# Remainders of the float32r splits on another engine in the attention phases, and query stacks built by copies

## The chip, the cores and the metric

One core of a Trainium2 chip runs the whole program. The metric is the device time of one execution in microseconds; the kernel before takes 1898.29 us (median of three runs, 1894.59 to 1900.06).

## What is computed

Two layers of a transformer trunk. Each layer has 512 latent and 256 context tokens of width 1024, one input projection whose columns go to four head groups (A: windowed attention with a sink, B: differential attention, C: retention in both directions, D: neighbourhood attention on a grid), one output projection, and a squared-ReLU MLP. Shift, scale and gate of every norm come from a linear map of the condition.

```python
hx = rms_norm(x, p['norm1_g']) * (1 + sc1x) + sh1x
(lw_q, ..., ln_v) = split_in(hx @ p['w_in'])          # the same for the context tokens
out_w = window_attention(q, k, v, k_c, v_c, p['a_sink'])
out_f = rms_norm(diff_attention(q, k, v, k_c, v_c, lam), p['b_subln_g']) * (1 - lambda_init)
out_r = rms_norm(o_f + flip(o_b), p['c_gn_g']) * gate
out_n = neighbourhood_attention(q, k, v, k_c, v_c, p['d_rpb'])
x = x + g1x * (concatenate([out_w, out_f, out_r, out_n]) @ p['w_out'])
h2 = rms_norm(x, p['norm2_g']) * (1 + sc2x) + sh2x
x = x + g2x * (square(relu(h2 @ p['w_mlp1'])) @ p['w_mlp2'])
```

The second layer has no outputs for the context tokens, so its queries and its MLP run over 512 columns in place of 768.

## The kernel before, in words

Activations lie transposed in SBUF, features on partitions and tokens on columns, 768 to a tile. TensorE multiplies in float32r, a rounded form of float32, so a float32 operand is split into a rounded part `hi` and a remainder `lo`, and a product takes three matmuls: hi x hi, hi x lo, lo x hi (L315 to L317 in `gemm`). `split` (L274) makes the two: ScalarE copies the source into `hi` (L275), VectorE subtracts `hi` from the source into `lo` (L276). All callers of `split` share these two lines in the profile, so one tells them apart by the tiles: `wh`, `wl` for weights, `pth`, `ptl` for transposed probabilities, `sp` for group B's queries and keys, `oh`, `ol` for the attention outputs.

`wload` (L278) loads a 128x512 chunk of weights into `wr` (five buffers) on SP's queue, and splits it into `wh` and `wl` (four buffers each), with a priority 40 places ahead of the code around it. Every input tile has two chunks.

Queries and keys are stacked so that the parts lie above one another on the contraction axis. `qstack` (L594; groups A, C, D) puts a head's 64 rows of `hi` and 64 rows of `lo` into one tile: ScalarE writes one half (L599), VectorE the other (L600), both across partitions. `kstack` (L603) writes `hi` twice and `lo` twice: one half by ScalarE (L608) and VectorE (L610), the other half by a DMA from the first (`KCOPY`, L633, issued by SP at L634). Group B has four heads of 32 rows to a tile, and `stack32` (L617) splits the whole tile once and places all quarters by DMA, 16 copies to a stack.

A layer's attention consists of seven units, a0 b0 b1 c0 c1 d0 d1. A generator (`in_a` to `in_d`) yields a unit's input projections, another (`at_a` to `at_d`) its attention. `weave` (L106) runs through them: while a unit's attention is emitted, the projections of the next are mixed in, so far ahead as written in constants (`lead`, 0.25 to 0.6 of a unit). The first attention of a layer therefore follows its own projections directly, with a part of the next unit's projection emitted before it. `out_ac` (L1033), the output projection of six of the eight tiles, is the filling for the last unit. A scheduler takes what is emitted in order of priority and fixes the order on each engine when the kernel is built; at run time each engine and SP's queue work strictly in that order and wait at semaphores. All DMAs are issued by SP.

The tiles `zq` (five buffers of 128x768) hold what is short-lived: squares, a projection on its way, group B's `hi` and `lo`. `u3` (20 buffers) holds stacks and outputs. GpSimd is used for nothing. `mods_dve` makes the condition's products on VectorE beside the MLP.

Of the kernel before, what the change touches and what calls it, by code (L numbers as in the profile page):

```python
# [9 lines left out]
F32 = mybir.dt.float32  # L10
F32R = mybir.dt.float32r
AF = mybir.ActivationFunctionType
OP = mybir.AluOpType
# [66 lines left out]
PTB = 2  # L80
PSB = 2
POB = 1
ZQ = 5
U3 = 20
MID = 14
WPRI = 40
# [67 lines left out]
@with_exitstack  # L154
def body(ctx: ExitStack, tc, A):
    nc = tc.nc
    V, S, G, T, SY = nc.vector, nc.scalar, nc.gpsimd, nc.tensor, nc.sync

    cons = ctx.enter_context(tc.tile_pool(name="cons", bufs=1))
    main = ctx.enter_context(tc.tile_pool(name="main", bufs=1))  # L160
# [6 lines left out]
    def nm(p):  # L167
        cnt[0] += 1
        return f"{p}{cnt[0]}"
# [18 lines left out]
    for w in (128, 64, 32):  # L188
        t = cons.tile([128, 32], F32, name=f"gmean{w}")
# [5 lines left out]
    with tc.tile_pool(name="sp0", bufs=1) as sp0:  # L195
        t = sp0.tile([128, 3, 128], F32, name="spread0")
# [74 lines left out]
            V.scalar_tensor_tensor(sq[:, s:s + l], ap, EPS if eps else 0.0, sq[:, s:s + l], op0=OP.add, op1=OP.mult)  # L271
        V.scalar_tensor_tensor(sq[:, :n], sq[:, :n], -3.0, e3[:, :n], op0=OP.add, op1=OP.mult)

    def split(src, hi, lo):  # L274
        S.activation(hi, src, AF.Copy)  # L275
        V.tensor_tensor(lo, src, hi.bitcast(F32), op=OP.subtract)  # L276

    def wload(src, k0=0, k1=8, dst=None):  # L278

        res = []  # L280
        for a in range(k0, k1, 4):
            n = min(4, k1 - a)
            r = wp.tile([128, 512], F32, name=nm("wr"), tag="wr", bufs=WR)[:, :128 * n]
            SY.dma_start(out=r, in_=src[:, 128 * a:128 * a + 128 * n])
            if dst is not None:
                hi, lo = dst
            else:
                hi = wp.tile([128, 512], F32R, name=nm("wh"), tag="wh", bufs=WB)
                lo = wp.tile([128, 512], F32R, name=nm("wl"), tag="wl", bufs=WB)
            with tc.high_priority(offset=WPRI):  # L290
                split(r, hi[:, :128 * n], lo[:, :128 * n])
            res += [(hi[:, 128 * k:128 * k + 128], lo[:, 128 * k:128 * k + 128]) for k in range(n)]
        return res

# [30 lines left out]
    def u3r(p):  # L325
        return main.tile([128, 768], F32R, name=nm(p), tag="u3", bufs=U3)
# [135 lines left out]
    for L in range(DEPTH):  # L462
        last = L == DEPTH - 1
        nq = NX if last else NT
# [2 lines left out]
        rb = rowb[:, L, :]  # L467
        modc = modcs[L]


        att = ExitStack()
        ap_ = att.enter_context(tc.tile_pool(name=f"att{L}", bufs=1))
        if L == 0:
# [34 lines left out]
            order = [(c[0], int(c[1])) for c in LOADS.split()]  # L508
            for c in order[:AHEAD]:
                load(*c)  # L510
            order = order[AHEAD:]
            h = htiles()
            gs = gstile()
            y = acc1
# [76 lines left out]

        HALF = (slice(0, 64), slice(64, 128))

        def qstack(t, n):  # L594

            st = (u3r("qs"), u3r("qs"))
            for h, x in enumerate(st):
                a, b = HALF[h], HALF[1 - h]
                S.activation(x[a, :n], t[a, :n], AF.Copy)  # L599
                V.tensor_tensor(x[b, :n], t[a, :n], x[a, :n].bitcast(F32), op=OP.subtract)  # L600
            return st

        def kstack(t, n):  # L603

            st, lo = (u3r("ks"), u3r("ks")), (u3r("kl"), u3r("kl"))
            for h, (x, y) in enumerate(zip(st, lo)):
                a, b = HALF[h], HALF[1 - h]
                S.activation(x[a, :n], t[a, :n], AF.Copy)  # L608
                KCOPY(x[b, :n], x[a, :n])
                V.tensor_tensor(y[a, :n], t[a, :n], x[a, :n].bitcast(F32), op=OP.subtract)  # L610
                KCOPY(y[b, :n], y[a, :n])
            return st, lo

        def quarter(i):
            return slice(32 * i, 32 * i + 32)

        def stack32(t, n, order):  # L617

            parts = [main.tile([128, 768], F32R, name=nm("sp"), tag="zq", bufs=ZQ)[:, :n] for _ in range(2)]
            split(t[:, :n], *parts)  # L620
            st = [u3r("st") for _ in range(4)]
            for i, x in enumerate(st):
                for r, w in enumerate(order):
                    KCOPY(x[quarter(r), :n], parts[w][quarter(i)])
            return st

        def qstack32(t, n):
            return stack32(t, n, (0, 1, 0, 1))

        def kstack32(t, n):  # L630
            return stack32(t, n, (0, 0, 1, 1))

        def KCOPY(dst, src):  # L633
            SY.dma_start(out=dst.bitcast(F32), in_=src.bitcast(F32))  # L634
# [260 lines left out]
        def ctables(hd):  # L895

            lf, nlb = lg[:, hd:hd + 1], nlg[:, 4 + hd:5 + hd]
            tb = grptile()
            tx = ap_.tile([128, 2, 512], F32, name=nm("tx"), tag="grp", bufs=GRP)
            SY.dma_start(out=tb[:, 0:896], in_=A['dd'][:, 0:896])  # L900
            SY.dma_start(out=tx.rearrange("p t i -> p (t i)"), in_=A['dd'][:, 896:1920])
            tn = zm()
            V.tensor_scalar(tn[:, 0:128], tb[:, 384:512], 0.0, lf, op0=OP.max, op1=OP.mult)
            V.tensor_scalar(tb[:, 384:512], tb[:, 384:512], 0.0, nlb, op0=OP.min, op1=OP.mult)
            V.tensor_tensor(tb[:, 384:512], tb[:, 384:512], tn[:, 0:128], op=OP.add)
            S.activation(tb[:, 384:512], tb[:, 384:512], AF.Exp)
            V.tensor_tensor(tb[:, 384:512], tb[:, 384:512], ident, op=OP.add)
            S.activation(tb[:, 0:384], tb[:, 0:384], AF.Exp, scale=nlb)
            S.activation(tb[:, 512:896], tb[:, 512:896], AF.Exp, scale=lf)
            for t in range(2):  # L910
                tw = zm()
                SY.dma_start(out=tw[:, 0:512], in_=A['dd'][:, 1920 + 512 * t:2432 + 512 * t])
                S.activation(tw[:, 0:512], tw[:, 0:512], AF.Exp, scale=nlb)
                S.activation(tx[:, t], tx[:, t], AF.Exp, scale=lf)
                V.tensor_tensor(tx[:, t], tx[:, t], tw[:, 0:512], op=OP.add)
            return tb, tx

        def in_c(u):
# [114 lines left out]
        def out_ac():  # L1033

            osp = []
            for c in range(6):
                hi, lo = htile("oh"), htile("ol")
                split(of[c][:, :nq], hi[:, :nq], lo[:, :nq])
                osp.append((hi, lo))
            for m in range(8):  # L1040
                xr = u3("xr")
                SY.dma_start(out=xr[:, :nq], in_=xsrc[:, m, :nq])
                ps = yield from gemm(wload(A['wout'][L, m], 0, 6), osp, halves(nq))
                xnew[m] = u3("x")
                for p, s, l in ps:
                    V.scalar_tensor_tensor(xnew[m][:, s:s + l], p, modc[:, 16 + m, s // 512:s // 512 + 1], xr[:, s:s + l],
                                           op0=OP.mult, op1=OP.add)
                yield 0
# [6 lines left out]
        cost_at = {x: c * 1e3 for x, c in zip('abcd', [[CA0, CB0, CC0, CD0], [CA1, CB1, CC1, CD1]][L])}  # L1055
        weave(units, ins, ats, cost_in, cost_at, out_ac(), [[L0_0, L0_1, L0_2, L0_3, L0_4, L0_5, L0_6, L0_7], [L1_0, L1_1, L1_2, L1_3, L1_4, L1_5, L1_6, L1_7]][L], lambda: tc.high_priority(offset=BOOST))
        att.close()


        mlp = ExitStack()  # L1060
# [235 lines left out]
```

## Time and profile before

| | us |
|---|---|
| median of the runs | 1898.29 |
| the profiled execution | 1897.64 |
| its span, from first to last instruction | 1895.6 |
| TensorE busy, share of the span | 1843.1, 97% |
| VectorE | 1307.4, 69% |
| ScalarE | 973.4, 51% |
| GpSimd | 0.2 |

Layer 0's attention lies from about 60 to 545 us, its MLP up to 1105, layer 1's attention up to 1530 and its MLP up to the end. A row of the groups below names the engine (PE is TensorE, DVE VectorE, ACT ScalarE, POOL GpSimd, SPq SyncE's queue), the line, and the tile written <- the tiles read. Matmuls are pipelined and their ends are modelled, so a busy PE is not one at its peak. The granted clock of TensorE stands as a share of 2.4 GHz; its lower level is 1.2 GHz.

### The profile page before, as it was taken

To read this page: it belongs to the slowest core of one execution; us is meant where nothing else is said; L and a number is where in the kernel's file an instruction comes from. 1 tells how busy PE (TensorE), PEld (TensorE's weight loads), DVE (VectorE), ACT (ScalarE), POOL (GpSimd) and SP (SyncE) were. 2 spreads that over 40 slices of the span, in tenths; PEclk is the share of its full clock that TensorE was granted. 3 is DMA by queue.
4 is the path that set the end of the run, shared out by engine and by line. 5 is a ranking of instruction groups with operands and counts; after the bars stand their busy time and mean duration, and the time that the engine had idled before them with its cause. 6 is when DMAs were issued, how large, how long until landed. Compare 5 with 4: busy or idle time off the path is not lost.

```text
span 1895.6 us, 29665 instructions
## 1 busy us (share of the span) xinstructions
PE 1843.1 (97%) x10899; PEld 1519.8 (80%) x10899; DVE 1307.4 (69%) x3005; ACT 973.4 (51%) x1934; POOL 0.2 (0%) x4
## 2 busy tenths in 40 slices
PE   7998889999999999999999999999899999999999
PEld 3786667778878888888888777878677788989897
DVE  5788867788777847847847367898788764545453
ACT  4677656668654214223323356877577763334242
POOL 0000000000000000000000000000000000000000
PEclk8999989999999999999999999999899999999999
DMA  8324334432323523423422352332243223232322
GB/s 297 99 79 122 100 120 131 148 95 65 109 95 106 157 93 117 151 95 117 150 95 89 111 172 83 83 96 79 85 133 95 75 95 100 90 100 90 100 90 95
DMA packets 110417, 208.68 MB, mean 110 GB/s; under 512 B 14272, under 2 KB 20160, under 8 KB 110272
## 3 DMA queue, kind: packets, MB, share of 16 engines
q1 hardware_dynamic: 110272, 206.78, 34.7%
q8 instruction: 86, 1.41, 0.3%
q14 instruction: 59, 0.48, 0.1%
HBM read 182.09 MB, written 5.24 MB: 99 GB/s over the span
## 4 chain that ended last, share of the span: by engine, by line
PE 89%; ACT 5%; DVE 3%; DMA 2%; issue 1%; SPq 0%; ACTq 0%; DVEq 0%
PE mm L315 23%; PE mm L317 23%; PE mm L316 23%; PE ps L697 3%; PE po L703 2%; PE po L705 2%; PE ps L262 1%; PE ps L850 1%; PE pt L241 1%; ACT pth L275 1%; PE pt L257 1%; PE pt L869 1%; PE pt L798 1%; ACT P L856 1%; DMA zm<-in_dd_dram 1%
## 5 line engine op out<-in xcount | busy, mean ns | idle before, releaser
L275 ACT ACTIVATE wh<-wr 128x512 fp32r<-128x512 f32 (+1 forms) x414 | 252.9, 614 | 645.3 <-PE mm L316 605.0
L317 PE MATMUL mm<-hh,wl 128*128 128x512 f32 (+2 forms) x1680 | 548.8, 327 | 6.7 <-DVE wl L276 6.6
L315 PE MATMUL mm<-hh,wh 128*128 128x512 f32 (+2 forms) x1680 | 551.2, 328 | 3.0 <-ACT zq L651 1.7
L316 PE MATMUL mm<-hl,wh 128*128 128x512 f32 (+2 forms) x1680 | 549.8, 327 | 0.0
L276 DVE TENSOR_TENSOR wl<-wr,wh 128x512 fp32r<-128x512 f32 (+1 forms) x414 | 275.4, 667 | 162.4 <-ACT wh L275 156.4
L315 PEld LDWEIGHTS mm<-hh,wh 128*128 128x128 f32 x1680 | 318.3, 190 | 39.9 <-issue 7.6
L317 PEld LDWEIGHTS mm<-hh,wl 128*128 128x128 f32 x1680 | 318.9, 190 | 34.7 <-DVE wl L276 7.7
L316 PEld LDWEIGHTS mm<-hl,wh 128*128 128x128 f32 x1680 | 318.0, 189 | 28.1 <-issue 3.5
L316 PE MATMUL mm<-ml,wh 128*128 128x512 f32 (+1 forms) x768 | 273.2, 356 | 0.0
L315 PE MATMUL mm<-mh,wh 128*128 128x512 f32 (+1 forms) x768 | 272.7, 356 | 0.0
L317 PE MATMUL mm<-mh,wl 128*128 128x512 f32 (+1 forms) x768 | 272.4, 355 | 0.0
L316 PEld LDWEIGHTS mm<-ml,wh 128*128 128x128 f32 x768 | 145.2, 189 | 24.5 <-issue 4.5
L315 PEld LDWEIGHTS mm<-mh,wh 128*128 128x128 f32 x768 | 145.2, 189 | 21.9 <-issue 0.4
L317 PEld LDWEIGHTS mm<-mh,wl 128*128 128x128 f32 x768 | 145.1, 189 | 21.2 <-issue 1.2
L394 DVE SCALAR_TENSOR_TENSOR acc<-wm,silp,acc 128x512 f32<-128x512 f32 x196 | 138.9, 747 | 21.9 <-DMA wm<-in_wmod_dram 21.7
L1127 DVE SCALAR_TENSOR_TENSOR x<-mm,modc,x 128x512 f32<-128x512 f32 (+1 forms) x96 | 63.4, 660 | 116.6 <-PE mm L317 116.6
L703 PE MATMUL po<-pth,vv 128*128 128x256 f32 (+2 forms) x328 | 105.5, 328 | 8.9 <-ACT pth L275 8.1
L276 DVE TENSOR_TENSOR ptl<-pt,pth 128x512 fp32r<-128x512 f32 (+3 forms) x148 | 92.4, 630 | 27.9 <-ACT pth L275 26.4
L275 ACT ACTIVATE pth<-pt 128x512 fp32r<-128x512 f32 (+3 forms) x148 | 80.2, 547 | 32.2 <-PE pt L869 21.6
L1111 DVE TENSOR_TENSOR zq<-mm,nacc 128x256 f32<-128x256 f32 (+1 forms) x128 | 61.9, 484 | 44.5 <-PE mm L317 43.0
L703 PEld LDWEIGHTS po<-pth,vv 128*128 128x128 f32 x328 | 61.8, 189 | 32.3 <-ACT pth L275 24.0
L705 PE MATMUL po<-ptl,vv 128*64 128x256 f32 (+2 forms) x256 | 78.3, 318 | 2.9 <-DVE ptl L276 2.3
(251 smaller groups left out, 2701.3 us busy)
## 6 DMA issues: line engine op xcount, KB each, us to landing
wr<-in_w_dram SPq DMA_DIRECT2D x272, 256.0 KB, 2.6
wm<-in_wmod_dram SPq DMA_DIRECT2D x112, 256.0 KB, 2.8
wr<-in_win_dram SPq DMA_DIRECT2D x96, 256.0 KB, 3.0
wr<-in_wmodh_dram SPq DMA_DIRECT2D x48, 256.0 KB, 3.3
st<-sp SPq DMA_DIRECT2D x96, 96.0 KB, 2.2
w<-in_wmod_dram SPq DMA_DIRECT2D x16, 384.0 KB, 7.1
tx<-in_dd_dram SPq DMA_DIRECT2D x8, 512.0 KB, 4.4
zm<-in_dd_dram SPq DMA_DIRECT2D x16, 256.0 KB, 3.5
```

The costliest lines, as they stand in the source:

```text
L241: T.matmul(pj, lhsT=gmean[w], rhs=sq[:, 256 * j:256 * j + 256], start=True, stop=add is None)
L275: S.activation(hi, src, AF.Copy)
L276: V.tensor_tensor(lo, src, hi.bitcast(F32), op=OP.subtract)
L315: T.matmul(p, lhsT=wh, rhs=ah[:, s:s + l], start=(k == 0), stop=False)
L316: T.matmul(p, lhsT=wh, rhs=al[:, s:s + l], start=False, stop=False)
L317: T.matmul(p, lhsT=wl, rhs=ah[:, s:s + l], start=False, stop=(k == len(act) - 1))
L394: V.scalar_tensor_tensor(acc[:, v], r, sil[:, k, v:v + 1], acc[:, v], op0=OP.mult, op1=OP.add)
L697: T.matmul(o, lhsT=x, rhs=y, start=(i == 0), stop=(i == 1))
L703: T.matmul(po[:, c0:c0 + l], lhsT=vv[:, hh, t], rhs=ph, start=start, stop=stop)
L705: T.matmul(po[0:64, c0:c0 + l], lhsT=vv[:, hh, t, 0:64], rhs=pl, start=False, stop=False)
L1111: V.tensor_tensor(r[:, s:s + l], p[:, :l], y2[:, s:s + l], op=OP.mult)
L1127: V.scalar_tensor_tensor(xx, p, modc[:, 40 + m, s // 512:s // 512 + 1], xx, op0=OP.mult, op1=OP.add)
```

## The change

While a layer's attention phase is emitted, remainders are subtracted on GpSimd: of weights (`wrest`), of queries and keys of all groups, and of the attention outputs in `out_ac`. The sum in group C's tables (L915) moves too. In the MLP, and for the last two output tiles, VectorE keeps them, as it keeps those of probabilities and values. Queries and keys of groups A, C and D are now split as whole tiles into two `zq` tiles, and SP's copies put all parts in place: four for a query stack (none before), eight for a key stack (four before). Group B's stacks are built as before, but for the engine of the subtraction. `zq` has six buffers.

```diff
-ZQ = 5
+ZQ = 6
...
-    def split(src, hi, lo):
+    def split(src, hi, lo, eng=V):
         S.activation(hi, src, AF.Copy)
-        V.tensor_tensor(lo, src, hi.bitcast(F32), op=OP.subtract)
+        eng.tensor_tensor(lo, src, hi.bitcast(F32), op=OP.subtract)
+
+    wrest = [PL]
...
-                split(r, hi[:, :128 * n], lo[:, :128 * n])
+                split(r, hi[:, :128 * n], lo[:, :128 * n], wrest[0])
...
+        wrest[0] = PL
...
+        def parts_of(t, n):
+
+            hl = [main.tile([128, 768], F32R, name=nm("sp"), tag="zq", bufs=ZQ)[:, :n] for _ in range(2)]
+            split(t[:, :n], *hl, PL)
+            return hl
+
+        def stack(hl, n, r, order):
+
+            x, w = u3r("st"), r.stop - r.start
+            for i, o in enumerate(order):
+                KCOPY(x[w * i:w * i + w, :n], hl[o][r])
+            return x
+
         def qstack(t, n):
 
-            st = (u3r("qs"), u3r("qs"))
-            for h, x in enumerate(st):
-                a, b = HALF[h], HALF[1 - h]
-                S.activation(x[a, :n], t[a, :n], AF.Copy)
-                V.tensor_tensor(x[b, :n], t[a, :n], x[a, :n].bitcast(F32), op=OP.subtract)
-            return st
+            hl = parts_of(t, n)
+            return [stack(hl, n, r, (0, 1)) for r in HALF]
 
         def kstack(t, n):
 
-            st, lo = (u3r("ks"), u3r("ks")), (u3r("kl"), u3r("kl"))
-            for h, (x, y) in enumerate(zip(st, lo)):
-                a, b = HALF[h], HALF[1 - h]
-                S.activation(x[a, :n], t[a, :n], AF.Copy)
-                KCOPY(x[b, :n], x[a, :n])
-                V.tensor_tensor(y[a, :n], t[a, :n], x[a, :n].bitcast(F32), op=OP.subtract)
-                KCOPY(y[b, :n], y[a, :n])
-            return st, lo
+            hl = parts_of(t, n)
+            return [[stack(hl, n, r, (i, i)) for r in HALF] for i in range(2)]
...
         def qstack32(t, n):
-            return stack32(t, n, (0, 1, 0, 1))
+
+            hl = parts_of(t, n)
+            return [stack(hl, n, quarter(i), (0, 1, 0, 1)) for i in range(4)]
 
         def kstack32(t, n):
-            return stack32(t, n, (0, 0, 1, 1))
+            hl = parts_of(t, n)
+            return [stack(hl, n, quarter(i), (0, 0, 1, 1)) for i in range(4)]
...
-                V.tensor_tensor(tx[:, t], tx[:, t], tw[:, 0:512], op=OP.add)
+                PL.tensor_tensor(tx[:, t], tx[:, t], tw[:, 0:512], op=OP.add)
...
-                split(of[c][:, :nq], hi[:, :nq], lo[:, :nq])
+                split(of[c][:, :nq], hi[:, :nq], lo[:, :nq], PL)
...
         att.close()
+        wrest[0] = V
```

`V`, `S`, `PL` and `SY` are the queues of VectorE, ScalarE, GpSimd and SyncE.

## Rows read from the trace of the kernel before

**Rows 1.** Page, busy us (share of the span) and instructions of each engine.

```profile
PE 1843.1 (97%) x10899; PEld 1519.8 (80%) x10899; DVE 1307.4 (69%) x3005; ACT 973.4 (51%) x1934; POOL 0.2 (0%) x4
```

**Rows 2.** Busy time by stretch: us, engines (instructions), PEclk, DMA share, GB/s.

```profile
core 0: us, PE busy (x) PEld busy (x) DVE busy (x) ACT busy (x) POOL busy (x), PEclk, DMA share, GB/s
0.00:60.00 60.00, 47.49 (x302) 27.43 (x303) 35.72 (x165) 26.74 (x51) 0.20 (x4) 0.89 0.68 248
150.00:350.00 200.00, 180.48 (x1132) 137.66 (x1132) 153.89 (x441) 127.21 (x286) 0.00 (x0) 0.97 0.41 120
560.00:1100.00 540.00, 540.00 (x3023) 459.93 (x3022) 351.00 (x604) 171.28 (x282) 0.00 (x0) 1.00 0.36 116
1250.00:1400.00 150.00, 138.80 (x739) 107.06 (x738) 125.38 (x302) 102.03 (x204) 0.00 (x0) 0.97 0.33 94
...
235.00:255.00 20.00, 12.28 (x47) 7.81 (x46) 10.43 (x28) 7.75 (x15) 0.00 (x0) 0.66 0.40 116
1330.00:1350.00 20.00, 13.40 (x60) 9.86 (x58) 17.38 (x48) 12.61 (x26) 0.00 (x0) 0.83 0.22 62
```

**Rows 3.** Waits of PE, 150 to 350 us: total us, times, longest us.

```profile
PE po L703 <- ACT pth L275: 4.0, 7, 0.7
...
PE pt L869 <- DVE P L860: 2.5, 4, 0.8
PE ps L850 <- DVE sm L724: 2.0, 5, 0.5
PE po L705 <- DVE ptl L276: 1.8, 5, 0.6
```

**Rows 4.** Waits of PE, 1250 to 1400 us: the longest in total.

```profile
PE mm L317 <- DVE wl L276: 6.6, 2, 3.4
```

**Rows 5.** Instructions by line and shape: busy us, mean ns, then idle us before them.

```profile
L276 DVE TENSOR_TENSOR wl<-wr,wh 128x512 fp32r<-128x512 f32 x382 | 262.3, 688 | 157.6 <-ACT wh L275 153.1 <-PE po L703 0.2
L276 DVE TENSOR_TENSOR wl<-wr,wh 128x256 fp32r<-128x256 f32 x32 | 13.3, 420 | 4.8 <-ACT wh L275 3.4 <-issue 1.3
L600 DVE TENSOR_TENSOR qs<-zq,qs 64x768 fp32r<-64x768 f32 x12 | 11.4, 953 | 1.6 <-ACT qs L599 1.2
L600 DVE TENSOR_TENSOR qs<-zq,qs 64x512 fp32r<-64x512 f32 x12 | 8.2, 686 | 0.4
L610 DVE TENSOR_TENSOR kl<-zq,ks 64x768 fp32r<-64x768 f32 x20 | 19.0, 949 | 1.3 <-ACT ks L608 0.9
L915 DVE TENSOR_TENSOR tx<-tx,zm 128x512 f32<-128x512 f32 x16 | 10.8, 687 | 5.5 <-ACT zm L913 4.5 <-ACT tx L914 1.0
...
L608 ACT ACTIVATE ks<-zq 64x768 fp32r<-64x768 f32 x20 | 16.8, 841 | 2.6 <-DVE zq L667 2.3
```

**Rows 6.** Tile `ks`: SP's issue of a copy, ns min/median/max, and its landing.

```profile
L634 SPq DMA_DIRECT2D ks<-ks x20: 462/484/557, 71.7 to 1443.7; - x20
...
DMA to landing us min/median/max: 2.6/2.9/5.7
```

**Rows 7.** Waits of SP's queue, whole span: total us, times, longest us.

```profile
SPq L284 <- DVE wl L276: 728.4, 316, 17.6
...
SPq L634 <- ACT sp L275: 49.7, 5, 14.6
```

**Rows 8.** Waits of all engines, whole span: total us, times, longest us.

```profile
ACT wh L275 <- DMA wr<-in_win_dram: 9.6, 7, 3.3
...
PE po L703 <- ACT pth L275: 8.1, 15, 1.0
```

**Rows 9.** Instructions by line and shape: L860 of DVE.

```profile
L860 DVE SCALAR_TENSOR_TENSOR P<-P,sm,P 128x768 f32<-128x768 f32 x32 | 32.3, 1011 | 0.2
```

More of the change, by code (lines that the diff above doesn't have):

```diff
@@ L156, in body @@
     nc = tc.nc
-    V, S, G, T, SY = nc.vector, nc.scalar, nc.gpsimd, nc.tensor, nc.sync
+    V, S, PL, T, SY = nc.vector, nc.scalar, nc.gpsimd, nc.tensor, nc.sync
     cons = ctx.enter_context(tc.tile_pool(name="cons", bufs=1))
@@ L592, in body @@
         HALF = (slice(0, 64), slice(64, 128))
-        def qstack(t, n):
-            st = (u3r("qs"), u3r("qs"))
-            for h, x in enumerate(st):
-                a, b = HALF[h], HALF[1 - h]
-                S.activation(x[a, :n], t[a, :n], AF.Copy)
-                V.tensor_tensor(x[b, :n], t[a, :n], x[a, :n].bitcast(F32), op=OP.subtract)
-            return st
-        def kstack(t, n):
-            st, lo = (u3r("ks"), u3r("ks")), (u3r("kl"), u3r("kl"))
-            for h, (x, y) in enumerate(zip(st, lo)):
-                a, b = HALF[h], HALF[1 - h]
-                S.activation(x[a, :n], t[a, :n], AF.Copy)
-                KCOPY(x[b, :n], x[a, :n])
-                V.tensor_tensor(y[a, :n], t[a, :n], x[a, :n].bitcast(F32), op=OP.subtract)
-                KCOPY(y[b, :n], y[a, :n])
-            return st, lo
+        def parts_of(t, n):
[7 more added lines that the diff above has]
+            return x
+        def qstack(t, n):
+            hl = parts_of(t, n)
+            return [stack(hl, n, r, (0, 1)) for r in HALF]
+        def kstack(t, n):
+            hl = parts_of(t, n)
+            return [[stack(hl, n, r, (i, i)) for r in HALF] for i in range(2)]
         def quarter(i):
             return slice(32 * i, 32 * i + 32)
[L617 to L625, printed above, removed]
         def qstack32(t, n):
-            return stack32(t, n, (0, 1, 0, 1))
+            hl = parts_of(t, n)
+            return [stack(hl, n, quarter(i), (0, 1, 0, 1)) for i in range(4)]
         def kstack32(t, n):
-            return stack32(t, n, (0, 0, 1, 1))
+            hl = parts_of(t, n)
+            return [stack(hl, n, quarter(i), (0, 0, 1, 1)) for i in range(4)]
         def KCOPY(dst, src):
```

## The prediction

> **What bounds the kernel now.** I read the profile from the outside in. The table of busy times comes first: TensorE (PE) is busy for 1843.1 of 1895.6 us, VectorE (DVE) for 69%, and GpSimd (POOL) does nothing but four memsets [rows 1]. PE is therefore the bound, and the change takes not one matmul from it. All it can give back is time in which PE stands or runs slow: 1895.6 - 1843.1 = 52.5 us. The table by stretch tells where that lies. In the MLP (560 to 1100) PE is busy for 540.00 of 540 us, so nothing is to be had there, and the change leaves it alone. The two stretches in which group B's attention runs hold most of it: 200 - 180.48 = 19.5 us from 150 to 350 and 150 - 138.80 = 11.2 us from 1250 to 1400 [rows 2]. Another 12.5 us lie in the first 60 us, where inputs are still being loaded. In those two stretches DVE is busy for 153.89 of 200 (77%) and 125.38 of 150 (84%) [rows 2]: beside PE, the fullest engine.
>
> The waits of PE in those stretches name who was late. From 150 to 350: the split of transposed probabilities on ScalarE (ACT), 4.0 us; DVE's weighted difference L860, 2.5; its row maximum L724, 2.0; its remainder of the probabilities, 1.8 [rows 3]. From 1250 to 1400, two waits for a weight remainder wl on DVE make 6.6 us, 3.4 the longest [rows 4]. A weight remainder has its input long before; it came late because DVE works in order and stood behind row maxima of the attention.
>
> Last, the clock. In the 20 us from 235 PE has 0.66 of its clock, in the 20 us from 1330 0.83 [rows 2]; before each, PE had been standing (12.28 and 13.40 us busy of 20). With levels of 2.4 and 1.2 GHz that is 0.68 x 20 + 0.34 x 20 = 20 us at half speed.
>
> **What leaves DVE and ACT.** The subtractions of the hi/lo splits, counted from the loops. Weights in the attention phases: 24 input tiles of two chunks in two layers, and 16 output chunks, 112 of 128x512 at 0.688 us = 77.0 us, and 16 of 128x256 at 0.420 = 6.7. Queries L600: 11.4 + 8.2 = 19.6. Keys L610: 19.0. The tables' L915: 10.8 [rows 5]. Eight splits of group B and twelve of `out_ac` have the same forms: twelve of 128x768 at about 0.95 (L610's row, the same columns) and eight of 128x512 at 0.688 make 16.9 [rows 5]. Together 150 us of DVE's work. In 150 to 350 I count 24 of its 154 us, in 1250 to 1400 28 of 125, by the tiles that lie there at the same rows. ACT loses 24 + 20 half-height copies and gets 22 of full height with the same columns; a half of the keys takes 0.841 us [rows 5], so at most 22 x 0.841 = 18.5 us are saved.
>
> **What POOL gets.** By DVE's rows the same subtractions, full height instead of two halves, are 112 x 0.688 + 16 x 0.42 + 28 x 0.95 + 30 x 0.688 = 131 us [rows 5]. No row has POOL at arithmetic. From below I set DVE's 0.688 us for 128x512; no row excludes less, but nothing below counts on it. From above, POOL's time would fill the 910 us of the two attention phases (60 to 545 and 1105 to 1530) at 910 / 131 = 7 times DVE's rows, 4.8 us. I take twice DVE's row, 1.38 us for 512 columns and 1.9 for 768, as the value nearest to that row with room for a slower engine: 262 us, 29% of the phases. Weight remainders then come 0.7 us later than a free DVE would give them. What hides that: the four split tiles in the ring; one tile feeds 12 matmuls of 512 and 12 of 256 columns, and the MLP's row, 3023 matmuls mostly of these widths in 540 us, gives 0.179 us each [rows 2], so 4.3 us a tile. Without that cover 112 x 0.7 = 78 us would be lost.
>
> The Trainium skill (GPSIMD Engine Reference, section 3.1) measures 1.96 times VectorE's time for a two-input fp32 operation; by it an estimate is 1.35 us, and the sum would be the same.
>
> **What SP gets.** Twelve query stacks get four copies each in place of none, ten key stacks eight in place of four: 48 + 40 = 88 more DMAs. Each takes SP 0.484 us to issue and 2.9 us from issue to landing [rows 6]: 42.6 us of SP, and some 15 MB on 206.8 MB moved, 7%, while the DMA engines are 0.33 to 0.41 busy in these stretches [rows 2]. The stacks come later. A query stack before: two ACT and two DVE halves, overlapped, some 2.7 us. After: 0.84 (ACT) + 1.9 (POOL) + 4 x 0.484 + 2.9 = 7.6 us, 4.9 more. A key stack: 4.7 before at best (0.84 + 0.95 + 2.9), 9.5 after. Who waits for that: the unit's first scores. Units are woven so that the input projection of the next unit is done before the present attention ends; only the first unit of a layer has no attention before it. There, 0.35 of the next unit's projection is emitted ahead, one projection of 2 x 4.3 = 8.6 us, which covers 7.6 us barely. Bounds: 0 to 2 x 4.9 = 9.8 us; I take 1 us.
>
> A copy that waits at the head of SP's queue for POOL's remainder holds the loads behind it: weights, tables, masks. SP already waits at such copies, 49.7 us in five waits, 14.6 the longest, and at weight loads for a free buffer, 17.6 the longest [rows 7]. What this has cost: ACT waited seven times for a weight load in the whole run, 9.6 us, at most 3.3 [rows 8]. Five raw and four split tiles hide it (9 x 4.3 = 39 us of projection). I take nothing; the second rival holds the other end. On POOL, a stack's remainder waits for ACT's copy with weight remainders behind it, at most 0.84 us for what is queued on ACT just then: hidden by the same ring. The sixth `zq` buffer pays for one of the two that a stack now holds for some 10 us; if the ring runs short, ACT's next evacuation of a projection waits, and PE's third PSUM bank with it. The bounds are again 0 and the second rival's.
>
> **The sum.** (a) The two waits for wl, 6.6 us [rows 4]: POOL has no row maxima in front of them, but stacks' remainders; I take 5. (b) PE's waits for DVE in the two stretches: 2.5 + 2.0 + 1.8 [rows 3] and some 2 us in smaller ones of the same kinds, 8.3. DVE loses 24/154 = 16% and 28/125 = 22% of its work there. In proportion that gives 1.5 us, all of it 8.3; waiting in a queue at 80% load shrinks faster than the load, so I take half, 4.1. (c) Waits for ACT's split, 8.1 in the whole run, half of them here [rows 3, 8]: a third, 2.7, since ACT is relieved of little and gets its inputs from DVE sooner. (d) The clock: 20 us at half speed with PE two thirds busy cost some 6; if most of these drops go, 4. (e) Against it, 1 at the layers' starts. 5 + 4.1 + 2.7 + 4 - 1 = 14.8 us.
>
> The profiled execution took 1897.64 us, 2.0 more than its span, and 0.65 under the median of 1898.29. So 1897.6 - 14.8 = 1882.8, and against the median 1883.5: I write 1883.
>
> **The rivals.** First: the relief is off the path. For it: PE's gaps in B's attention also belong to a chain in which each link waits for the one before (scores, maximum, exponential, difference, transposition, split), and DVE idles for a fifth of the time there. Against it: the 6.6 us of [rows 4], which are queueing and nothing else. Then (a) is given back at the layers' starts, and the time is 1898, within 0.3% (5.7 us, about what a measurement of this kernel can tell from no change).
>
> Second, slower: the copies at SP's head. Twelve query stacks bring waits of SP that were not there; if each lets weights run out as the seven waits did, PE stands 12 x 1.4 = 17 us by their mean and 12 x 3.3 = 40 us by their longest [rows 8]. With (b) and (c) still won, 17 - 7 = 10 to 40 - 7 = 33 us are lost: 1908 to 1931, about 1915. It decides from the point at which SP reaches a query's copies with fewer weights in the rings than the stack takes, 7.6 us or two tiles. For it: the rings are seldom full in the attention, where loads wait 17.6 us for a buffer at one time and ACT for a load at another. Against it: 128 copies of group B already pass this way.
>
> Third, the two engines get in each other's way. POOL at 29% would meet DVE's operations with both inputs in SBUF: some 200 in the two phases (L860, the split of group C's products, the rotations L654 to L656, the norms L438 and L440), L860 the longest at 1.011 us [rows 9]. If one waits for the other to end, 200 x 0.29 x 0.69 (half a POOL operation) = 40 of the 150 us come back to DVE, and L860, on the late chain, loses 32 x 0.29 x 0.69 = 6.4 us directly. (b) and (c) shrink by 27%, 1.8: 14.8 - 6.4 - 1.8 = 6.6 us are left, 1891. The Trainium skill (SBUF — State Buffer, section "Who interferes with whom") states this as a rule: a VectorE instruction with two SBUF inputs and a GpSimd instruction that reads SBUF lock each other out for the whole instruction. Nothing here shows it, with POOL idle.
>
> **How the numbers follow.** Forecast 0.50, third rival 0.10, first 0.15, second 0.25. Faster by over 0.3%: 0.50 and most of the third, 0.58. Within: 0.15 and the rest of the third, 0.17. Slower: 0.25. The range: down to all that PE stands in the two stretches, 30.7 [rows 2], the clock's 6, and 5 for short stands that matmul ends, which are modelled, hide: 1898 - 42 = 1856. Up to the second rival's middle, 1915, which leaves out some 1 in 8 above.
>
> **What would show it.** wl, the stacks and tx stand on POOL at 1.2 to 2 us for 512 columns; over 3 us the cover is in doubt. DVE's busy time falls by 150 us to about 1157 (less if the third rival holds: then L860 and L654 show longer means or gaps before them). PE's waits for wl between 1250 and 1400 are gone, and PEclk there is 1. The MLP keeps its 540 us. The second rival would show as ACT waiting for loads of `win` above 20 us, and SP at L634 for POOL. I am wrong if PE's idle time in the two stretches stays at 30 us, or if new waits for the stacks (L697) stand at the start of units.

## The result, and the profile after

The changed kernel takes 1921.82 us (median of four runs, 1917.40 to 1923.66) against 1897.48 for the kernel before, measured beside it: 24.3 us more, a ratio of 1.0125, with a 95% interval of 1.0102 to 1.0149. The forecast was 1883 us, in a range of 1856 to 1915. The time went the other way, and out of the range.

First the busy times from the page of the changed kernel, which answer to [rows 1].

```profile
span 1919.1 us, 29993 instructions
PE 1853.4 (97%) x10899; PEld 1517.4 (79%) x10899; DVE 1239.1 (65%) x2797; ACT 955.2 (50%) x1912; POOL 261.1 (14%) x190
```

GpSimd got 261.1 us of work; the forecast said 262. VectorE should have fallen to 1157 us, and stands at 1239.1. The stretches [rows 2]:

```profile
150.00:350.00 200.00, 183.26 (x1103) 137.83 (x1101) 146.51 (x424) 123.71 (x282) 39.55 (x26) 0.94 0.44 127
350.00:500.00 150.00, 137.55 (x799) 106.51 (x800) 94.59 (x203) 94.89 (x200) 53.71 (x37) 1.00 0.41 120
560.00:1100.00 540.00, 539.06 (x3029) 455.39 (x3028) 361.54 (x630) 180.15 (x310) 0.00 (x0) 1.00 0.36 113
1250.00:1400.00 150.00, 145.66 (x842) 116.14 (x843) 126.46 (x337) 109.73 (x228) 48.72 (x33) 1.00 0.40 112
```

In the two stretches on which the forecast was built PE's idle time did fall, from 19.5 to 16.7 us in the first and from 11.2 to 4.3 us in the second. The first stretch gained nothing by it: its granted clock fell from 0.97 to 0.94, which with levels of 2.4 and 1.2 GHz is 24 of the 200 us at the lower one in place of 12, and PE ran 1103 matmuls there in place of 1132. From 350 to 500, where the attention of groups C and D in layer 0 runs, PE now stands for 12.5 us. The kernel before had 2.3 there:

```profile
350.00:500.00 150.00, 147.66 (x893) 119.23 (x892) 123.72 (x299) 116.58 (x249) 0.00 (x0) 1.00 0.30 91
```

Over the whole run PE stands 13.2 us longer (65.7 us in place of 52.5) and is busy 10.3 us longer with the same 10899 matmuls.

When layer 0's last attention output is written, the changed kernel is 21.4 us behind (529.4 us against 508.0, the ends in the two traces), and at the end 23.5. In between it is 29.8 us behind at layer 1's first attention matmul (1201.5 against 1171.7) and 20.6 at layer 1's last attention output: layer 1's attention wins back what the stretch before it loses.

The waits of PE from 350 to 500 us name what is late there (columns as in [rows 3]). In the kernel before, the waits listed for this stretch were two kinds for ScalarE, 2.1 us in all.

```profile
PE po L704 <- DVE ptl L276: 4.1, 4, 2.1
PE mm L318 <- POOL ol L276: 2.4, 3, 1.3
PE po L701 <- DVE ptl L276: 1.6, 3, 0.8
PE ps L696 <- DVE of L970: 1.5, 2, 1.3
```

VectorE is less busy in this stretch than before, 94.59 us against 123.72, and yet PE waits for it. The instructions by line and shape show why; the first rows are GpSimd's, the rest VectorE's, and they answer to [rows 5, 9]. Two rows of the kernel before stand ahead of them.

```profile
L276 DVE TENSOR_TENSOR ptl<-P,pth 128x512 fp32r<-128x512 f32 x48 | 32.8, 683 | 3.4 <-ACT pth L275 3.2
L655 DVE TENSOR_TENSOR zq<-zq,rt 128x512 f32<-128x512 f32 x14 | 9.6, 683 | 0.0
```

```profile
L276 POOL TENSOR_TENSOR wl<-wr,wh 128x512 fp32r<-128x512 f32 x110 | 152.5, 1391 | 1076.2 <-ACT wh L275 991.7 <-PE ps L849 44.6 <-PE ps L696 16.5
L276 POOL TENSOR_TENSOR sp<-zq,sp 128x768 fp32r<-128x768 f32 x22 | 41.8, 1903 | 85.4 <-ACT sp L275 44.1 <-PE mm L319 30.3 <-PE ps L696 6.4
L276 DVE TENSOR_TENSOR ptl<-pt,pth 128x512 fp32r<-128x512 f32 x116 | 79.0, 687 | 41.0 <-ACT pth L275 39.7 <-PE po L702 0.5
L276 DVE TENSOR_TENSOR ptl<-P,pth 128x512 fp32r<-128x512 f32 x48 | 39.8, 834 | 10.8 <-ACT pth L275 10.6
L859 DVE SCALAR_TENSOR_TENSOR P<-P,sm,P 128x768 f32<-128x768 f32 x32 | 35.0, 1094 | 0.3
L852 DVE TENSOR_SCALAR sm<-sm 128x2 f32<-128x2 f32 x40 | 14.3, 365 | 0.2
L654 DVE TENSOR_TENSOR zq<-zq,rt 128x512 f32<-128x512 f32 x14 | 12.8, 915 | 0.0
```

The remainder of transposed probabilities that reads `pt`, which is in PSUM, keeps its 687 ns. The same subtraction in group C reads `P`, in SBUF, and takes 834 ns in place of 683. L859 (before L860, 1011 ns) takes 1094, and L654 (before L655, 683 ns) 915. The row L852 is two numbers per partition and took 159 ns before (then L853); now 365. The view of tile `sm` gives the shortest, median and longest of these forty in ns, first of the kernel before, then of the changed one:

```profile
L853 DVE TENSOR_SCALAR sm<-sm x40: 140/159/169, 170.3 to 1349.1; 128x2 f32<-128x2 f32 x40
```

```profile
L852 DVE TENSOR_SCALAR sm<-sm x40: 148/160/1802, 173.1 to 1368.8; 128x2 f32<-128x2 f32 x40
L858 DVE TENSOR_SCALAR sm<-sm,nlam,l x40: 255/270/275, 178.8 to 1372.8; 128x1 f32<-128x1 f32 x40
```

The median has not moved and the longest is 1802 ns, nearly as long as a GpSimd subtraction of 768 columns. The instruction is not slower: sometimes it stands until one of GpSimd's is over. Eleven of the forty take 289 ns or more in the trace; each of them began while GpSimd worked, and each ends 23 to 31 ns after GpSimd's instruction. This is the picture of the third rival. The Trainium skill (SBUF — State Buffer, section "Who interferes with whom") says that whoever issues first keeps the shared ports for its whole instruction while the other is fully blocked, and that `tensor_scalar` in some shapes uses both port pairs; the trace agrees, with 1802 ns against a median of 160, and with L858, one column wide, that stays at 275 or less (four of its forty began while GpSimd worked).

Over the whole run the durations of VectorE's instructions sum to 1468.1 us before and 1377.3 after. The work taken away was 150 us, so what is left got 59 us longer.

### The profile page after: what moved, and what is told of

It is laid out like the page before. It is cut to its first block, busy times and chain, and to the rows that moved or that the text cites. A ratio compares the mean times of both kernels' runs of the same rounds, so it can differ in the third digit from the quotient of the medians.

```text
span 1919.1 us, 29993 instructions
## 1 busy us (share of the span) xinstructions
PE 1853.4 (97%) x10899; PEld 1517.4 (79%) x10899; DVE 1239.1 (65%) x2797; ACT 955.2 (50%) x1912; POOL 261.1 (14%) x190
## 5 line engine op out<-in xcount | busy, mean ns | idle before, releaser
L276 POOL TENSOR_TENSOR wl<-wr,wh 128x512 fp32r<-128x512 f32 x126 | 165.1, 1317 | 1095.7 <-ACT wh L275 1004.4
L276 DVE TENSOR_TENSOR wl<-wr,wh 128x512 fp32r<-128x512 f32 (+1 forms) x288 | 193.9, 673 | 144.0 <-ACT wh L275 139.8
L696 PE MATMUL ps<-st,st 128*128 128x256 f32 (+2 forms) x400 | 104.0, 329 | 5.3 <-DVE P L961 2.2
```

The source lines that it names most:

```text
L276: eng.tensor_tensor(lo, src, hi.bitcast(F32), op=OP.subtract)
L696: T.matmul(o, lhsT=x, rhs=y, start=(i == 0), stop=(i == 1))
```

## The experiments

The theory at this point: GpSimd's reads hold VectorE up ("the hold"), and since the held instructions lie in the attention's chains, the time grows. Its rivals: copies that delay SP's queue (the forecast's second rival), weights and stacks that come late because GpSimd is slow, a worse order from the scheduler, and a relief that was worth nothing. Each ratio is to the kernel before on the same chip, with its 95% interval. A kernel whose work is put on other engines, or that has another number of buffers, gets a new order from the scheduler, so it differs by more than its edit; where a kernel keeps the order of the kernel before on PE, VectorE, ScalarE and SP, this is said.

**Weights alone.** The changed kernel, its sixth buffer included, with the functions for the stacks as they were before the change; stacks, tables and outputs have their remainders on VectorE. Against the changed kernel, the stacks left out of the cut:

```diff
-                PL.tensor_tensor(tx[:, t], tx[:, t], tw[:, 0:512], op=OP.add)
+                V.tensor_tensor(tx[:, t], tx[:, t], tw[:, 0:512], op=OP.add)
...
-                split(of[c][:, :nq], hi[:, :nq], lo[:, :nq], PL)
+                split(of[c][:, :nq], hi[:, :nq], lo[:, :nq], V)
```

> The weights' remainders alone are on GpSimd (128 subtractions, some 165 us); stacks, tables and output remainders are as in the kernel before, with six zq buffers. Theory L (while GpSimd reads SBUF, VectorE's operations with all operands in SBUF wait, so the relief comes back as longer operations): VectorE's rows with all operands in SBUF get longer as in the changed kernel (the remainder of group C's products 683 to about 830 ns), and the time is within 8 us of before. Theory C (copies that come late and stand at the head of SP's queue cost it): without them the relief is left alone, so 10 to 20 us faster than before. Theory O (another order of instructions, fixed when the kernel is built, costs it): anything within 25 us, with no row longer.

1908.13 against 1898.55 us: 1.0046 [1.0028, 1.0064], 9.6 us more. The weights, the largest part of the relief, lose by themselves.

**Copies alone.** All stacks by copies, all remainders on VectorE. Against the changed kernel:

```diff
-    wrest = [PL]
+    wrest = [V]
-            split(t[:, :n], *hl, PL)
+            split(t[:, :n], *hl, V)
...
```

> Queries and keys are split as whole tiles and all parts are placed by copies, as in the changed kernel, but every remainder stays on VectorE, so GpSimd is idle. Theory C: the 88 extra copies cost 12 to 30 us against before. Theory L: within 6 us of before, since nothing reads SBUF on GpSimd; VectorE's rows keep their lengths (683 ns). Theory O: anything within 25 us.

1893.04 us: 0.9976 [0.9967, 0.9985], 5.5 us less. The second rival is not the cause.

**The stacks' remainders on GpSimd.** As the last, but `split(t[:, :n], *hl, PL)`.

> As the kernel with copies alone, but the remainders of queries and keys (30 subtractions, some 53 us) are on GpSimd; weights, tables and outputs stay on VectorE. Theory C: the stacks come about 1 us later still than with VectorE, 12 to 30 us slower than before. Theory L: 53 of the 261 us of GpSimd, so a fifth of the changed kernel's stretched rows and at most 5 us slower than before. Theory O: anything within 25 us.

1906.78 us: 1.0051 [1.0030, 1.0072], 8.2 us more, so 13.7 us more than with the same copies on VectorE. GpSimd is busy for only 51.5 us here. Two causes are mixed in this run, the hold and stacks that come later; it does not part them. At the price that the next run gives, 0.157 us for each us of GpSimd, the hold would be 8 of the 13.7 us, an estimate, and 6 would be left for the later stacks and the new order.

**Subtractions that nobody reads.** The kernel before; beside each of the 128 splits of weights in the attention phases, GpSimd subtracts `hi` from itself into a tile of its own. VectorE keeps all its work, nobody reads what GpSimd makes, and the order on the other engines is that of the kernel before. Only ScalarE waits for GpSimd, three times and 3.7 us in all, where a buffer of `wh` is still being read.

```diff
                 split(r, hi[:, :128 * n], lo[:, :128 * n])
+                if extra[0]:
+                    x = wp.tile([128, 512], F32R, name=nm("xt"), tag="xt", bufs=1)
+                    G.tensor_tensor(x[:, :128 * n], hi[:, :128 * n].bitcast(F32), hi[:, :128 * n].bitcast(F32), op=OP.subtract)
```

> The kernel before with all its work in place, and 128 GpSimd subtractions more, one behind each weight chunk's rounded part in the attention phases, whose results nobody reads; the order on all other engines is that of before, instruction by instruction. Theory L: VectorE's rows with all operands in SBUF get longer by a fifth on average (683 to about 800 ns), and since VectorE keeps its full load, 8 to 30 us slower than before. Theories C and O: the same as before within 4 us.

1923.24 us: 1.0133 [1.0118, 1.0148], 24.7 us more, as much as the whole change, from work whose results nothing uses. Its page and three of its rows by line and shape:

```profile
PE 1854.5 (97%) x10899; PEld 1519.6 (79%) x10899; DVE 1354.0 (71%) x3005; ACT 973.8 (51%) x1934; POOL 157.1 (8%) x132
L276 DVE TENSOR_TENSOR wl<-wr,wh 128x512 fp32r<-128x512 f32 x382 | 277.1, 727 | 157.7 <-ACT wh L275 153.7
L276 DVE TENSOR_TENSOR ptl<-P,pth 128x512 fp32r<-128x512 f32 x48 | 35.2, 734 | 2.3 <-ACT pth L275 2.1
L660 DVE TENSOR_TENSOR zq<-zq,rt 128x512 f32<-128x512 f32 x14 | 13.2, 940 | 0.0
```

The same 3005 instructions of VectorE keep it busy for 46.6 us longer than in [rows 1]. Neither the order, nor late weights, nor copies are left as an explanation of these 24.7 us, and ScalarE's 3.7 us are not it either: the next run has 12.8 us of such waits and no loss. Per us of GpSimd's work the kernel pays 24.7 / 157.1 = 0.157 us.

**Writes in their place.** The same places, a copy of one column and four memsets each (the unread tile is of plain float32 here); same order.

```diff
-                    G.tensor_tensor(x[:, :128 * n], hi[:, :128 * n].bitcast(F32), hi[:, :128 * n].bitcast(F32), op=OP.subtract)
+                    i = G.tensor_copy(x[:, 0:1], hi[:, 0:1].bitcast(F32))
+                    for _ in range(4):
+                        G.memset(x[:, :128 * n], 0.0)
```

> The kernel before with GpSimd work that nobody waits for, at the same 128 places as in the run with extra subtractions, and in the same order on every other engine; but the work is a copy of one column and four memsets of the chunk, which write SBUF and read nothing. Theory R (VectorE is held by GpSimd's reads): the 24.7 us of the extra subtractions shrink to under 5, and the rows of VectorE with two SBUF inputs (the rotation's product 683, the weights' remainder 688) keep their lengths. Theory W (any GpSimd work on SBUF holds VectorE): as with the subtractions or more, 15 to 30 us slower than before, with the same rows longer.

1901.04 against 1900.54 us: 1.0003 [0.9992, 1.0013], no difference, though GpSimd is busy for 303.3 us, longer than in the changed kernel. The rows:

```profile
L276 DVE TENSOR_TENSOR ptl<-P,pth 128x512 fp32r<-128x512 f32 x48 | 32.8, 684 | 3.8 <-ACT pth L275 3.6
L867 DVE SCALAR_TENSOR_TENSOR P<-P,sm,P 128x768 f32<-128x768 f32 x32 | 32.4, 1011 | 0.2
L860 DVE TENSOR_SCALAR sm<-sm x40: 141/160/541, 170.1 to 1355.5; 128x2 f32<-128x2 f32 x40
```

Operations with two inputs keep their lengths; only one-input operations like the last row stand now and then for about the length of a memset, 541 ns at most in this row. So what holds the operations with two inputs is that GpSimd reads, not that it runs or writes. The same section of the Trainium skill says that two-input operations contend with GpSimd instructions that read SBUF, not with those that only write; the trace agrees, with 684 ns here and 734 beside the subtractions.

**Twice as many.** Two unread subtractions in each place; same order.

> As the run with extra GpSimd subtractions that nobody reads, but two behind each weight chunk in place of one, so some 315 us of GpSimd in place of 157, in the same order on all other engines. Theory L (VectorE held by GpSimd): the cost grows with GpSimd's time, 40 to 60 us slower than before against 24.7 with one. A cost that comes from something that the first extra instruction brings (a start, a buffer) would stay near 25.

1952.59 us: 1.0276 [1.0256, 1.0297], 52.0 us more for 310.1 us of GpSimd, 0.168 each. Over these two amounts the price is about proportional, without a sign of saturation or of a free allowance.

**The sixth buffer alone.** The kernel before with `ZQ = 6`.

> The kernel before with six zq buffers in place of five and nothing else. If the sixth buffer or the other order that it brings makes the 5.5 us that the kernel with copies alone gained, this is 3 to 8 us faster than before; if the gain is that of the copies (19 us less on VectorE and 17 on ScalarE), it is within 3 us of before. Theory O (order alone moves the time by tens of us) would show here too.

1890.11 us: 0.9951 [0.9932, 0.9971], 10.4 us less. The one line of the change that the forecast counted at nothing is its only gain that survives. The new order that comes with the buffer (382 of VectorE's 3005 instructions stand at another place) is part of this; the run does not part the two. The copies thus seem to cost something: 0.9976 with them against 0.9951 without, about 5 us, with intervals that touch.

**Copies, and weights on GpSimd in layer 1 only.** Against the run with the copies alone:

```diff
-        wrest[0] = V
+        wrest[0] = PL if L == 1 else V
```

> Copies for all stacks with every remainder on VectorE, as in the kernel with copies alone, but the weights' remainders of the second layer's attention phase on GpSimd (64 subtractions). In the kernel with all weights' remainders on GpSimd the first layer lost some 16 us against before and the second won some 6. If the second layer bears the exchange, this is 3 to 10 us faster than copies alone; if GpSimd's reads cost there too, as theory L has it with VectorE relieved by about as much, it is within 4 us of copies alone.

1891.07 us: 0.9957 [0.9943, 0.9971], 3.6 us below the copies alone by the ratios, at the edge of what the intervals tell apart.

**The sixth buffer, and weights on GpSimd in layer 1 only.** The same edit of `wrest` with the old stacks.

> The kernel before with six zq buffers, and the remainders of weights on GpSimd in layer 1 only; old stacks. With copies, the same step (layer 1 only) was worth 0.9957 against 0.9976, 3.6 us, and layer 1 is where the waits for wl stood. If the relief there outweighs the hold whatever the stacks: 10.4 + 3.6 = 14 us under the kernel before, 0.9926, the fastest of all. If the two only cancel, as the marks of the changed kernel's layer 1 had it (90.8 us of stands against 89.7): as the sixth buffer alone, 0.995. If layer 1 too pays half of the 19 us that the weights' remainders cost in both layers: 0.9995.

1892.60 against 1898.98 us: 0.9963 [0.9949, 0.9976]. This is the second of the expected cases: in layer 1 gain and price cancel. Nothing beats the sixth buffer alone among the kernels that compute everything.

**Copies in place of the unread subtractions.** One tile read, not two; same order.

```diff
-                    G.tensor_tensor(x[:, :128 * n], hi[:, :128 * n].bitcast(F32), hi[:, :128 * n].bitcast(F32), op=OP.subtract)
+                    G.tensor_copy(x[:, :128 * n], hi[:, :128 * n])
```

> The kernel before, and in the 128 places of the unread subtractions a GpSimd copy of hi to the same unread tile in their stead: one tile read, not two. The order on the other engines is that of the kernel before. If any read of SBUF by GpSimd holds VectorE up, the time grows by 0.157 us for each us that GpSimd works: with the 1.39 us of a subtraction, +25; with half of it, +12; and VectorE's rows with all operands in SBUF get longer as there. If only an operation with two inputs does, the time stays at the kernel before, within 0.15%, and VectorE's rows keep their lengths.

1906.66 us: 1.0036 [1.0021, 1.0052], 7.7 us more, neither the 0 of one theory nor 0.157 x 102 = 16 of the other. GpSimd's row, and two of VectorE's:

```profile
L296 POOL CAST xt<-wh 128x512 fp32r<-128x512 f32 x110 | 90.6, 824 | 1376.9 <-ACT wh L275 1376.3
L276 DVE TENSOR_TENSOR ptl<-P,pth 128x512 fp32r<-128x512 f32 x48 | 32.9, 685 | 3.1 <-ACT pth L275 2.8
L276 DVE TENSOR_TENSOR wl<-wr,wh 128x512 fp32r<-128x512 f32 x382 | 268.9, 705 | 159.2 <-ACT wh L275 155.2
```

With 102.1 us of GpSimd the price is 0.075 per us, half of a subtraction's. Some rows grow (wl 688 to 705), others don't (ptl 683 to 685). The trace shows that a copy holds as a subtraction does, but is over sooner. The 19 wl subtractions of 128x512 that are lengthened here end 0.54 us after GpSimd's copy, the 23 beside the unread subtractions 0.55 us after GpSimd's subtraction; the longest take 1143 and 1536 ns. Of the 48 ptl subtractions only three began beside a copy. The durations of VectorE's instructions grow by 16.9 us in sum, 0.166 for each us of GpSimd, against 45.0 us and 0.286 beside the subtractions. In that proportion the price would be 0.091, an estimate; the interval of the ratio, 4.0 to 9.9 us, allows 0.039 to 0.097. So a difference in kind between copy and subtraction is not shown.

**Weights, with five buffers.** The kernel before, with the remainders of weights on GpSimd in both attention phases, and nothing else of the change.

```diff
-                split(r, hi[:, :128 * n], lo[:, :128 * n])
+                split(r, hi[:, :128 * n], lo[:, :128 * n], wrest[0])
...
+        wrest[0] = PL
```

> The kernel before, with the remainders of weights on GpSimd in both attention phases and nothing else of the change: five zq buffers and the old stacks, as before. So it is the run on weights without the sixth buffer. VectorE loses 84 us of work; GpSimd gets some 166. If hold and relief add up: GpSimd's reads cost 0.157 us for each of its us, +26, as the unread subtractions did, and the relief of VectorE gives back 5 to 8 us, in the forecast's proportion (84 of 150 us of its 14.8): +18 to +21, ratio 1.0095 to 1.011. The same follows from the run on weights with six buffers (+8.7) and the run with the sixth buffer alone (-10.4): +19. If relief was worth nothing at all: +26 or more. If the sixth buffer's gain is not to be had once VectorE is relieved, the two runs on weights are alike: about +9, 1.0046, and then the relief is worth 17 us.

1910.52 us: 1.0062 [1.0045, 1.0078], 11.5 us more for 170.4 us of GpSimd. At 0.157 the reads cost 26.8 us, so the relief is worth 15: more than the 8 of the forecast's proportion. The +19 that followed from adding up the runs with the sixth buffer is refuted: those two gains do not add.

**The relief alone.** The same kernel, with nearly all of GpSimd's reads taken away. It leaves out the weights' remainders of the attention phases: zeros stand in their place, and the matmuls on them stay.

```diff
-                split(r, hi[:, :128 * n], lo[:, :128 * n], wrest[0])
+                if wrest[0] is V:
+                    split(r, hi[:, :128 * n], lo[:, :128 * n])
+                else:
+                    S.activation(hi[:, :128 * n], r, AF.Copy)
+                    PL.tensor_tensor(lo[:, 0:1], r[:, 0:1], hi[:, 0:1].bitcast(F32), op=OP.subtract)
+                    for _ in range(2):
+                        PL.memset(lo[:, :128 * n].bitcast(F32), 0.0)
```

> The run on weights with five buffers, with GpSimd's subtraction replaced by one over a single column and two memsets of the whole tile: the tile wl is ready as late after wh as there (0.36 + 2 x 0.53 = 1.4 us in place of 1.41), for the same readers, but GpSimd reads next to nothing. The weights' remainders of the attention phases are left out (zeros in their place), so the time is that of the kernel with VectorE relieved of 84 us and of nothing put in its way: what the forecast had assumed. If the hold is the whole cause, by difference (+11.8 of the run on weights, less the 24.7 to 26 that GpSimd's reads cost): 13 to 14 us under the kernel before, ratio 0.993, with VectorE's rows at their old lengths. By the forecast's own proportion (84 of 150 us of 14.8) 8 us under, 0.9956. If the relief lies off the path, as the forecast's first rival has it: 0.998 to 1.001. If weights that come from GpSimd late are what costs: above 1.002.

1881.87 against 1897.96 us: 0.9917 [0.9900, 0.9934], 16.1 us less. From the page, the stretches and the rows by line and shape:

```profile
PE 1842.2 (98%) x10899; PEld 1515.4 (81%) x10899; DVE 1244.3 (66%) x2877; ACT 973.0 (52%) x1934; POOL 163.0 (9%) x388
150.00:350.00 200.00, 188.55 (x1145) 141.93 (x1146) 146.73 (x429) 128.31 (x287) 23.22 (x54) 0.95 0.41 119
1250.00:1400.00 150.00, 148.94 (x820) 116.98 (x819) 123.70 (x297) 111.10 (x224) 32.86 (x69) 1.00 0.38 107
L276 DVE TENSOR_TENSOR ptl<-P,pth 128x512 fp32r<-128x512 f32 x48 | 32.9, 685 | 6.0 <-ACT pth L275 5.8
L869 DVE SCALAR_TENSOR_TENSOR P<-P,sm,P 128x768 f32<-128x768 f32 x32 | 32.4, 1013 | 0.3
```

PE's idle time in the two stretches falls from 30.7 us to 11.45 + 1.06 = 12.5, and VectorE's two-input rows have their old lengths. Between this run and the last, GpSimd has about the same time (163.0 and 170.4 us) and wl of 512 columns is ready about as late after wh (medians of 1.44 and 1.38 us). The order is not quite the same, and no run shows by itself what zeros do to the time of a matmul; but 22.1 of the 29.8 us between the two spans are time in which PE stands (58.1 and 36.0 us). What differs in kind is that GpSimd reads; it makes 11.5 + 16.1 = 27.6 us, and 27.6 / 170.4 = 0.162 per us is the price that the unread subtractions had.

## Why the prediction was wrong, point by point

**What bounds the kernel: right.** PE's stands beside a full VectorE were worth having. The last run has 16.1 us from the weights' part of the relief alone, where the sum had 14.8 for all parts; the first rival, a relief off the path, is refuted by it. The sum erred on the low side with the waits: PE's idle time fell from 52.5 to 36.0 us. The sign of failure that the forecast named did not show in the changed kernel: PE's idle time in the two stretches fell from 30.7 to 21.1 us. The loss stands elsewhere, between 350 and 500 us and in PE's longer busy time.

**The clock (d): wrong.** Four us of gain were counted. With the relief alone PE is busy for 1842.2 us in place of 1843.1, and the clock from 150 to 350 is 0.95 in place of 0.97: at most 0.9 us came back. In the changed kernel the slow stretch near 1330 us is gone (1.00 from 1250 to 1400, as forecast), but from 150 to 350 the clock fell to 0.94, and PE is busy 10.3 us longer. The forecast's figures for PE's standing "before each" drop (12.28 and 13.40 us of 20) are those of the slow stretches themselves, so they do not show what came before.

**GpSimd's price: right.** 1391 ns and 1903 ns were forecast as 1.38 and 1.9 us, and 261.1 us as 262. The cover for slower remainders held: PE's waits for GpSimd's wl are 1.3 us from 150 to 350, and none is listed from 1250 to 1400, where [rows 4] had 6.6 us. Not covered were the attention outputs' remainders `ol`: PE waits 2.4 us for them. The Trainium skill (GPSIMD Engine Reference, section 3.1) had 1.96 times VectorE's time, and an estimate of 1.35 us came of it; the trace agrees, with 1391 ns against 688, 2.02 times.

**What leaves VectorE: half wrong.** Busy time fell by 68 us, not 150. Of the missing 82, 59 are longer instructions. The rest is arithmetic of the forecast's own: row sums count instructions that overlap twice (1468.1 us by rows, 1307.4 by the page [rows 1]), so a difference of rows is more than the difference of busy times. The run with the relief alone shows it nearly without a hold: VectorE's durations sum to 77 us less, and the page has 63 less.

**The copies (second rival): right to doubt, wrong in price.** Copies seem to cost about 5 us, not the 17 to 40 at which this rival was priced before its offsets. The first of its signs did not show: ScalarE's waits for loads of `win` are 9.1 us against 9.6 [rows 8]. The second did, SP at the copies for GpSimd, 17.4 us in 18 waits; and SP's waits there for ScalarE's `sp`, which now stands for all groups, grew from 49.7 us [rows 7]:

```profile
SPq L633 <- ACT sp L275: 62.4, 14, 9.2
SPq L633 <- POOL sp L276: 17.4, 18, 1.4
ACT wh L275 <- DMA wr<-in_win_dram: 9.1, 8, 2.2
```

**The layers' starts.** One us was taken, 9.8 was the upper bound. Layer 0's first attention matmul starts at 83.53 us before and 90.05 after, 6.5 later, two thirds of that bound; at the first unit's last output (175.5 and 180.6) 5.2 are left. With the copies alone it starts 2.8 later than before, with the stacks' remainders on GpSimd 5.4.

**The sixth buffer: wrong.** Counted at nothing, it takes 10.4 us off the kernel before. By which wait it does so, and how much of it is the new order, is not settled.

**The third rival: this step failed.** The sum has no term for it: that VectorE stands while GpSimd reads was counted at nothing, because nothing showed it with POOL idle, and as a rival it was priced at 8.2 us. Its mechanism is the cause, and this price was wrong in two places. The first is the list of instructions. Over the some 200 that were listed the growth is 22 us, 0.11 each in place of the 0.29 x 0.69 = 0.20 us expected (means: the norms 0.05, L859 0.08, ptl 0.15, L654 0.23). The other 37 us lie with instructions that were not listed: 16 with the short operations on `sm` (0.21 for each of L852), 8 with group C's tables `gp`, the rest scattered. So 59 us came back in place of 40. The larger error is the second: only L860 was put on the path, so that 40 us of longer instructions were to cost 6.4 + 1.8 = 8.2 us. In the run with unread subtractions the durations grow by 45.0 us in sum (1468.1 to 1513.1) and the time by 24.7, so 0.55 of each us arrives. For 261.1 us of GpSimd, at 0.157, this makes an estimate of 41 us of hold. With 8.2 put right to 41, the forecast's 14.8 of gain becomes 26 of loss, and 1924; measured were 1921.82. This closeness is partly luck, since the sixth buffer's 10.4 us and the weights' 16.1 were not in the sum either.

Why a us of hold costs so much more than a us of relief gives (16.1 / 77 = 0.21) can only be argued: a weight's remainder mostly has the ring's cover, so its removal frees VectorE rather than a chain, while a hold falls on the operations within the attention's chains as often as on others.

**The pieces.** From the medians, each against its own kernel before: sixth buffer -10.4; copies +4.9 (-5.5 less -10.4); stacks' remainders +13.7 (8.2 less -5.5); weights' remainders with six buffers +20.0 (9.6 less -10.4). The sum is +28.2; the change has +24.3, and the 3.9 between them lie with tables, outputs and what does not add up. For something does not: weights' remainders cost 11.5 us with five buffers and 20.0 with six. Perhaps relief and sixth buffer win the same stands; that was not shown.

The forecast gave the third rival a chance of 0.10, with the remark that nothing shows it while POOL is idle. But rows by which to weigh it were there: the tiles that [rows 5, 9] name tell, for the instructions that they show, whether all inputs are in SBUF.

## What to carry to other kernels

Before moving elementwise work from VectorE to GpSimd, count which VectorE instructions that will run beside it have all their operands in SBUF or are short ones like L852, and which of them lie in a chain: here each us of a two-input GpSimd operation cost 0.16 us of the whole, and 84 us of relief were worth 16. Work that only writes was free here: 256 us of memsets, with 47 us of one-column copies, made no difference that the interval shows. Time each edit of a bundle alone, buffer counts too: the one extra buffer, with the order that it brings, was worth 10.4 us and was hidden in a change that lost 24.3.

## What the runs showed of the hardware that was not expected

The hold reaches operations of two numbers per partition: L852 has a median of 160 ns and a longest of 1802. GpSimd's memsets hold such an operation for about their own length (541 ns at most in the row shown), but two-input operations not at all (684 ns, 1011 ns). A held instruction ends at a fixed distance behind GpSimd's: in the changed kernel 23 to 31 ns for the operations on `sm`, 0.55 us for the subtractions ptl. The hold goes the other way too: GpSimd's wl subtractions of 512 columns have a median of 1292 ns and a longest of 2388, and of the 22 that take 1465 ns or more, twenty end 1.13 to 1.16 us after the VectorE operation during which they began. A GpSimd copy costs half of a subtraction per us, 0.075 against 0.157, and is over sooner. And the price per us is about the same for 310 us of GpSimd's work, 16% of the span, as for 157 (0.168 and 0.157).
